# Two MLP phases of a hybrid backbone: sums of products nested in PSUM, stored operand combinations, and phase two product by product

## The chip, the core and the metric

The kernel runs on one core of a Trainium2 chip. The metric is the device time in microseconds (us) of one execution, as the median of three runs. TensorE (PE) multiplies, VectorE (DVE), ScalarE (ACT) and GpSimd (POOL) work element by element, and SyncE (SP) issues nearly all transfers between HBM and the on-chip SBUF, in the order of its own queue. PSUM is the memory in which TensorE accumulates.

## The reference, cut to what matters

Two layers over 1280 tokens (256 of a prompt, 1024 of a sample), width 1024, all in fp32. A layer is a mixer and an MLP with 4096 hidden units and a squared ReLU. Shift, scale and gate of either token group come from a modulation vector.

```python
def _modulation(cvec, w, b):
    m = jax.nn.silu(cvec) @ w + b
    return jnp.split(m[:, None, :], N_MOD, axis=-1)

def _mlp(h, w1, w2):
    return jnp.square(jax.nn.relu(h @ w1)) @ w2
...
        hp = _rmsnorm(xp, norm_mlp[l]) * (1.0 + mp[4]) + mp[3]
        hs = _rmsnorm(xs, norm_mlp[l]) * (1.0 + ms[4]) + ms[3]
        xp = xp + mp[5] * _mlp(hp, mlp_w1[l], mlp_w2[l])
        xs = xs + ms[5] * _mlp(hs, mlp_w1[l], mlp_w2[l])
    y_prompt = _rmsnorm(xp, norm_final)
    y_sample = _rmsnorm(xs, norm_final)
```

Layer 0 has the "even" mixer (windowed attention and a gated recurrence), layer 1 the "odd" one (Fourier and long convolutions). The change leaves both as they are, but for the order in which the odd mixer's first product takes its row tiles.

## The kernel before

**Precision.** Every large fp32 product is three products of rounded operands: an operand is split into `h` (rounded to fp32r) and `l` (the rest), and hh, hl and lh are summed. The split (L300, L303) is a cast on ScalarE and a subtraction on VectorE or GpSimd.

**Seven products.** Both matrix products of the MLP are cut into 2 x 2 blocks and done with seven block products instead of eight (Strassen-Winograd): "11", "21", "T1", "T2", "T3", "22" and "T4" name them, and also the combination of blocks that each one multiplies. One side's combinations are built from the activations, the other's from the weights (`wset`: additions on GpSimd in raw weight tiles `wr`, then `wtile` L802 splits each into `wt`). Weights are loaded as blocks of 512 KB into `wr`, of which there are two buffers, as there are of `wh` and `wl`.

**Phase 1** (L909 to L932), hidden activations: 16 steps j; each takes the seven products of 24 matmuls of 128 x 320 (`product`, L846), each product in a PSUM pair of its own. The sums of products are made outside of PSUM: ScalarE copies "11" and "T1" out (L857, L922), VectorE adds "21", "T2", "T3", "22" and "T4" (L860, L921, L924, L926, L929), GpSimd adds twice in SBUF (L923, L925). VectorE then squares the positive part of 1280 columns twice (L927, L930), and two rows of 640 KB go to the scratch `uscr`. A filler is pulled once per j: in layer 0 it is `modulation` for seven vectors, which multiplies rows of the modulation weights (`mt`) by the conditioning on VectorE, 224 instructions of L382 with a running sum.

**Phase 2** (L1021 to L1053), back to the width: seven chunks of 512 hidden units. For each, four rows `ur` are loaded back, `ops` builds and splits the seven combinations (tiles `o` and `oT`; additions on GpSimd, splits on ScalarE and VectorE), and for two halves `ms` of the columns the seven products run: 2 x 12 matmuls (L1034) into a PSUM pair each. Each pair is added to an accumulator `acc` in SBUF by VectorE (L1040). After the last chunk `merge` adds the seven accumulators up. The eighth chunk (512 hidden units) is a classic product (`proj`, L692), which adds into the residual `xm`; in layer 1 its columns go in two parts, with the final norm of the first part beside the second.

**What sets the order.** The program is written in the order in which loops and generators yield; a scheduler with a simulated timeline then sets the order of each engine's queue. Within a queue the instructions run in that order, and each waits for what its operands and its buffers need.

## Time and profile before

| | us |
|---|---|
| median of three runs | 3344.59 (3343.64 to 3347.43) |
| span of the profiled execution | 3345.9 |
| layer 0: steady part of phase 1 | 866 to 1240 |
| layer 0: phase 2 / classic chunk | 1261.6 to 1680 / to 1739.1 |
| layer 1: start and phase 1 | 2405.4 to 2846.8 |
| layer 1: phase 2 / classic chunk / tail | 2846.8 to 3264.7 / to 3327.8 / to 3345.9 |

| engine | busy us | share of the span |
|---|---|---|
| TensorE | 2960.5 | 88% |
| VectorE | 2512.5 | 75% |
| GpSimd | 1406.4 | 42% |
| ScalarE | 1225.1 | 37% |

Times within the kernel count from the start of the span. The shares are means over stages with different limits, so they don't tell which engine a stage waits for; for that the stages are read one by one, by windows, by the chain of waits and by what ended an engine's idle time. The granted clock of TensorE is 1.00 at its full 2.4 GHz; its mean over the span is 0.943.

### The profile page before, as it was taken

To read this page: it belongs to the slowest core of one execution; us is meant where nothing else is said; L and a number is where in the kernel's file an instruction comes from. 1 tells how busy PE (TensorE), PEld (TensorE's weight loads), DVE (VectorE), ACT (ScalarE), POOL (GpSimd) and SP (SyncE) were. 2 spreads that over 40 slices of the span, in tenths; PEclk is the share of its full clock that TensorE was granted. 3 is DMA by queue.
4 is the path that set the end of the run, shared out by engine and by line. 5 is a ranking of instruction groups with operands and counts; after the bars stand their busy time and mean duration, and the time that the engine had idled before them with its cause. 6 is when DMAs were issued, how large, how long until landed. Compare 5 with 4: busy or idle time off the path is not lost. (4 is left out here: it accounts for less than half of the span.)

```text
span 3345.9 us, 46730 instructions
## 1 busy us (share of the span) xinstructions
PE 2960.5 (88%) x18190; PEld 2716.9 (81%) x18190; DVE 2512.5 (75%) x3172; ACT 1225.1 (37%) x2032; POOL 1406.4 (42%) x912
## 2 busy tenths in 40 slices
PE   6799978897999998989799998887979999899977
PEld 3577767796988887989778876777979999898976
DVE  6886798648999987887983257875686656788896
ACT  5556757634111125333233332322432222533322
POOL 3530054524433336555630025543244344555563
PEclk8899989998999998999899998898989999999988
DMA  6363232341445443132331235546212223323232
GB/s 237 115 235 111 99 126 81 128 163 60 167 161 167 161 167 111 64 101 70 101 139 37 82 121 176 182 145 208 101 70 86 102 97 125 109 70 97 68 131 95
DMA packets 133336, 407.03 MB, mean 122 GB/s; under 512 B 14886, under 2 KB 29622, under 8 KB 133116
## 3 DMA queue, kind: packets, MB, share of 16 engines
q1 hardware_dynamic: 121596, 362.10, 31.6%
q0 software_dynamic: 11520, 41.95, 4.2%
q8 instruction: 144, 2.36, 0.3%
q14 instruction: 76, 0.62, 0.1%
HBM read 306.70 MB, written 97.29 MB: 121 GB/s over the span
## 5 line engine op out<-in xcount | busy, mean ns | idle before, releaser
L846 PE MATMUL pd<-BT,wt 128*128 128x320 f32 x3072 | 474.9, 314 | 42.5 <-ACT BT L764 21.6
L805 ACT CAST wt<-wr 128x512 fp32r<-128x512 f32 x360 | 221.2, 620 | 770.3 <-PE pd L1034 233.3
L846 PEld LDWEIGHTS pd<-BT,wt 128*128 128x128 f32 x3072 | 463.5, 192 | 48.1 <-ACT BT L764 22.6
L1034 PE MATMUL pd<-oT,wt 128*128 128x320 f32 x2688 | 427.8, 318 | 64.5 <-DVE acc L1040 54.5
L1034 PEld LDWEIGHTS pd<-oT,wt 128*128 128x128 f32 x2688 | 413.3, 195 | 72.7 <-issue 31.1
L846 PE MATMUL pd<-B,wt 128*128 128x320 f32 x2304 | 364.0, 315 | 35.2 <-DVE u L926 14.9
L846 PEld LDWEIGHTS pd<-B,wt 128*128 128x128 f32 x2304 | 349.4, 192 | 41.5 <-ACT wt L805 16.9
L1034 PE MATMUL pd<-o,wt 128*128 128x320 f32 x2016 | 324.7, 319 | 42.5 <-DVE acc L1040 25.8
L1034 PEld LDWEIGHTS pd<-o,wt 128*128 128x128 f32 x2016 | 310.5, 196 | 51.5 <-issue 24.6
L1040 DVE TENSOR_TENSOR acc<-acc,pd 128x640 f32<-128x640 f32 x336 | 270.2, 812 | 84.1 <-PE pd L1034 83.9
L300 DVE TENSOR_TENSOR wt<-wr,wt 128x512 fp32r<-128x512 f32 x276 | 265.8, 965 | 61.7 <-ACT wt L805 61.6
L923 POOL TENSOR_TENSOR u<-ut,u 128x640 f32<-128x640 f32 x32 | 55.0, 1719 | 413.0 <-ACT u L922 277.2
L300 POOL TENSOR_TENSOR ur<-ur 128x640 f32<-128x640 f32 x84 | 165.3, 1979 | 111.7 <-DVE o L300 69.5
L300 POOL TENSOR_TENSOR wt<-wr,wt 128x512 fp32r<-128x512 f32 x84 | 133.6, 1590 | 164.3 <-ACT wt L805 164.3
L300 POOL TENSOR_TENSOR wr<-wr 128x512 f32<-128x512 f32 x120 | 196.9, 1641 | 8.0
L692 PE MATMUL pb<-hh,wl 128*128 128x258 f32 (+1 forms) x720 | 191.9, 369 | 0.0
L692 PE MATMUL pb<-hh,wh 128*128 128x258 f32 (+1 forms) x720 | 191.5, 368 | 0.5 <-ACT hh L643 0.3
L692 PE MATMUL pb<-hl,wh 128*128 128x258 f32 (+1 forms) x720 | 191.5, 367 | 0.0
L303 ACT CAST wh<-wr 128x1024 fp32r<-128x1024 f32 x74 | 77.5, 1048 | 195.8 <-PE pd L692 79.8
L725 POOL TENSOR_TENSOR nacc<-nacc,nsq 128x640 f32<-128x640 f32 (+2 forms) x36 | 60.3, 1675 | 210.2 <-ACT nsq L724 210.1
L692 PEld LDWEIGHTS pb<-hh,wh 128*128 128x128 f32 x720 | 121.9, 190 | 27.9 <-issue 6.5
L692 PEld LDWEIGHTS pb<-hh,wl 128*128 128x128 f32 x720 | 121.9, 191 | 25.8 <-issue 6.0
(536 smaller groups left out, 6419.2 us busy)
## 6 DMA issues: line engine op xcount, KB each, us to landing
wr<-in_w_dram SPq DMA_DIRECT2D x136, 512.0 KB, 3.6
uscr<-u SPq DMA_DIRECT2D x64, 640.0 KB, 3.3
ur<-uscr SPq DMA_DIRECT2D x64, 640.0 KB, 4.9
tab<-in_dft_dram POOLq DMA_DIRECT2D x79, 512.0 KB, 4.7
mt<-in_mt_dram SPq DMA_DIRECT2D x112, 256.0 KB, 3.0
mw<-in_mw_dram SPq DMA_DIRECT2D x40, 512.0 KB, 4.7
x<-in_x_dram SPq DMA_DIRECT2D x16, 640.0 KB, 8.6
xmid<-x SPq DMA_DIRECT2D x32, 320.0 KB, 2.1
```

What stands on the lines that cost most here:

```text
L300: eng.tensor_tensor(o, x, y, ALU.subtract)
L303: S.copy(hi, src)
L692: T.matmul(ps[c][:, 0:N], w[wi][:, sl], hs[k][hi][:, c0:c0 + N], start=(ki == 0 and pi == 0), stop=(ki == nk - 1 and pi == 2))
L725: (V if last else G).tensor_tensor(s.acc[:, c0:c1], s.acc[:, c0:c1], sq, ALU.add)
L805: S.copy(t[:, 0], src)
L846: T.matmul(ps[:, c, 0:NQ], w[:, wi, 128 * k:128 * k + 128], B[n][k][:, hi_, NQ * c:NQ * c + NQ], start=(k == 0 and pi == 0), stop=(k == 3 ...
L923: G.tensor_tensor(u0[:, hi], t, u1[:, hi], ALU.add)
L1034: T.matmul(ps[:, z, 0:NQ], w[:, wi, sl], B2[n, k][:, hi_, NQ * z:NQ * z + NQ], start=(k == 0 and pi == 0), stop=(k == 1 and pi == 2))
L1040: V.tensor_tensor(d, d, ps[:, :, 0:NQ], ALU.add)
```

## The change

**Phase 1.** A product may be accumulated onto another one's PSUM pair (`onto`). The pair x takes "11", then "T2", "T3" and "T4" on top of it, and is read after each; z takes "T1" and then "22"; "21" has a pair of its own. VectorE adds "21", the sum after "T3" and the sum after "22"; ScalarE copies x after "11" and after "T2" and z after "T1", and takes the squared ReLU of two quarters in two passes (`act2`); VectorE squares the other two. The combinations that phase 2 multiplies are formed here (two subtractions on VectorE, two on GpSimd), and `keep` stores seven of them per j, 320 KB each, in `uscr`.

**Phase 2.** The loop goes product by product over all 4096 hidden units: eight steps `kk` for each of "11", "T2", "T3", "T4", "21", "T1" and "22". A step loads 640 KB of the stored combination, splits it (1280 elements a partition), loads one to three blocks of weights (T2: 3; T3 and T1: 2; the others: 1), combines them on GpSimd (in T2 also on VectorE), splits them (1024 elements) and runs 48 matmuls into four PSUM pairs, which are all of PSUM. "T2", "T3" and "T4" accumulate on "11", and "22" on "T1". After the eighth step of a product the four pairs are added to the residual through the gate (`addto`). `acc`, `merge` and the classic chunk are gone. In the last layer the squares for the final norm are taken in pieces, and the norm's end and the scaling of all eight tiles come after the last product, in two halves of 640 columns.

**Modulation** of the seven vectors goes to TensorE: 224 matmuls of 32 x 256 in fp32 and 56 that gather their rows, still as phase 1's filler in layer 0; its weights come in tiles of two per 512 KB, in the buffers of `tmp`, now six for four.

The three places in the engines' queues are these. A name in brackets is the engine or the DMA queue whose semaphore an instruction waits on; a number behind a name is that of its buffer.

TensorE in phase 1 of layer 1, a steady j, before: `BT2` and `BT1` are the operands of "T2" and "T1", `B21` that of "21", `pd` the PSUM pair.

```order
L846 MATMUL pd_23693<-B213_20211,wt_23594 128x320 x6
L846 MATMUL pd_23724<-BT20_20349,wt_23629 128x320 [waits DVE_49,Activation_49]
L846 MATMUL pd_23724<-BT20_20349,wt_23629 128x320 x5
L846 MATMUL pd_23724<-BT21_20359,wt_23629 128x320 x6
L846 MATMUL pd_23724<-BT22_20370,wt_23629 128x320 x6
L846 MATMUL pd_23724<-BT23_20380,wt_23629 128x320 x6
L846 MATMUL pd_23753<-BT10_20386,wt_23661 128x320 [waits Activation_49]
L846 MATMUL pd_23753<-BT10_20386,wt_23661 128x320 x3
L846 MATMUL pd_23753<-BT10_20386,wt_23661 128x320 [waits DVE_49]
L846 MATMUL pd_23753<-BT10_20386,wt_23661 128x320
```

After, the same place:

```order
L831 MATMUL pd_21326<-BT13_19990,wt_21225 128x320 x6
L831 MATMUL pd_21384<-B210_19780,wt_21293 128x320 [waits PE_49,Activation_49]
L831 MATMUL pd_21296<-BT20_19938,wt_21260 128x320 [waits Activation_49]
L831 MATMUL pd_21296<-BT20_19938,wt_21260 128x320 x3
L831 MATMUL pd_21296<-BT20_19938,wt_21260 128x320 [waits DVE_49]
L831 MATMUL pd_21296<-BT20_19938,wt_21260 128x320
L831 MATMUL pd_21296<-BT21_19948,wt_21260 128x320 x6
L831 MATMUL pd_21296<-BT22_19959,wt_21260 128x320 x6
L831 MATMUL pd_21296<-BT23_19969,wt_21260 128x320 x6
L831 MATMUL pd_21384<-B210_19780,wt_21293 128x320 x3
L831 MATMUL pd_21384<-B210_19780,wt_21293 128x320 [waits DVE_49]
```

Before, each product goes to a `pd` of its own, one after the other. Now "T2" goes onto the pair `pd_21296` that "11" filled, behind a wait for ScalarE's copy of it, and "T1" stands between the two; "21" has `pd_21384`.

VectorE within phase 2 of layer 1, before: L1040 empties PSUM, L300 splits the next chunk's operands.

```order
L1040 TENSOR_TENSOR acc<-acc,pd 128x640
L300 TENSOR_TENSOR oT_26848<-ur,oT_26848 128x640
L1040 TENSOR_TENSOR acc<-acc,pd 128x640
L300 TENSOR_TENSOR oT_26852<-ur,oT_26852 128x640
L300 TENSOR_TENSOR ur<-ur 128x640
L1040 TENSOR_TENSOR acc<-acc,pd 128x640
L300 TENSOR_TENSOR ur<-ur 128x640
L1040 TENSOR_TENSOR acc<-acc,pd 128x640
L300 TENSOR_TENSOR oT_26887<-ur,oT_26887 128x640
L1040 TENSOR_TENSOR acc<-acc,pd 128x640
L300 TENSOR_TENSOR oT_26893<-ur,oT_26893 128x640
```

After, in product "T2" of layer 1: `s` is the combination of weights, `ol` and `wt` the second parts of the splits.

```order
L295 TENSOR_TENSOR s_24395<-s_24395,wq 128x1024
L295 TENSOR_TENSOR wt<-s_24395,wt 128x1024
L295 TENSOR_TENSOR ol<-ur,oh 128x1280
L295 TENSOR_TENSOR s_24462<-s_24462,wq 128x1024
L295 TENSOR_TENSOR wt<-s_24462,wt 128x1024
L295 TENSOR_TENSOR ol<-ur,oh 128x1280
L295 TENSOR_TENSOR s_24529<-s_24529,wq 128x1024
```

Before, each addition out of PSUM stands behind a subtraction of the next chunk's operands. Within a product nothing is left that reads PSUM; the evacuations stand between two products.

SyncE within phase 2 of layer 1, before: `ur` are rows of activations, `wr` blocks of weights.

```order
L811 DMA wr_24602<-in_w2_dram 128x1024 [waits DMAHW5_49,Pool_49]
L811 DMA wr_24858<-in_w2_dram 128x1024 [waits DMAHW2_49,DVE_49]
L811 DMA wr_24860<-in_w2_dram 128x1024 [waits DMAHW3_49,Pool_49]
L979 DMA ur_25071<-uscr_100 128x1280 [waits DMAHW6_49,PE_49]
L979 DMA ur_25073<-uscr_100 128x1280 [waits DMAHW7_49,PE_49]
L979 DMA ur_25075<-uscr_100 128x1280 [waits DMAHW0_49,DVE_49,Pool_49]
L979 DMA ur_25077<-uscr_100 128x1280 [waits DMAHW1_49,DVE_49,Pool_49]
L811 DMA wr_25110<-in_w2_dram 128x1024 [waits DMAHW4_49,DVE_49]
```

After, in product "T2" of layer 1: `wq` is a third block of weights in another pool of buffers.

```order
L1014 DMA ur_24322<-uscr_99 128x1280 [waits DMAHW3_49,PE_49]
L955 DMA wq_24266<-in_w2_dram 128x1024 [waits DMAHW4_49]
L955 DMA wr_24262<-in_w2_dram 128x1024 [waits DMAHW1_49,Pool_49]
L955 DMA wr_24264<-in_w2_dram 128x1024 [waits DMAHW2_49]
L1014 DMA ur_24389<-uscr_99 128x1280 [waits DMAHW7_49,DVE_49,PE_49]
L955 DMA wq_24333<-in_w2_dram 128x1024 [waits DMAHW0_49]
L955 DMA wr_24329<-in_w2_dram 128x1024 [waits DMAHW5_49,Pool_49]
L955 DMA wr_24331<-in_w2_dram 128x1024 [waits DMAHW6_49]
```

Before, 4 loads of `ur` and 4 of `wr` serve a chunk of 336 matmuls. Now one `ur`, two `wr` and one `wq` serve a step of 48, and the first of two `wr` waits for GpSimd.

The diff, cut to its core:

```diff
+        for i in which:
+            mss = []
+            for jj in range(2):
+                ps = tbank()
+                for h in range(2):
+                    for kk in range(2):
+                        ws = []
+                        for z in range(2):
+                            w = tmp("mw", (128, 2, 256))
+                            ld(w.rearrange("p k c -> p (k c)"), a["mw"][l, 4 * i + 2 * jj + h, kk, :, 512 * z:512 * z + 512])
+                            ws.append(w)
+                        for g in range(4):
+                            T.matmul(ps[32 * g:32 * g + 32, 256 * h:256 * h + 256], st[:, 4 * kk + g, :], ws[g // 2][:, g % 2, :],
+                                     start=kk == 0, stop=kk == 1)
                         yield
-        for i in which:
-            m = mod[l][i]
-            V.tensor_tensor(m, macc[:, i, 0], macc[:, i, 1], ALU.add)
-            V.tensor_tensor(m, m, mb[:, l, 8 * i:8 * i + 8].unsqueeze(2).to_broadcast([128, 8, 2]), ALU.add)
-        yield
+                ms = tmp("ms")
+                S.copy(ms, ps)
+                mss.append(ms)
+            p2 = tbank()
+            for c in range(8):
+                T.matmul(p2[:, 2 * c:2 * c + 2], mss[c // 4][:, 128 * (c % 4):128 * (c % 4) + 128], sel, start=True, stop=True)
+            V.tensor_tensor(mod[l][i], p2[:, 0:16].rearrange("p (c s) -> p c s", s=2),
+                            mb[:, l, 8 * i:8 * i + 8].unsqueeze(2).to_broadcast([128, 8, 2]), ALU.add)
...
+        def product(n, w, onto=None):
+            ps = pbank() if onto is None else onto
...
+                                 start=(onto is None and k == 0 and pi == 0), stop=(k == 3 and pi == 2), skip_group_check=True)
...
+        def keep(n, j, src):
+            ld(uscr[UN[n], j // 2, :, j % 2], src)
+
+        def act2(dst, src):
+            S.activation(dst, src, AF.Relu)
+            S.activation(dst, dst, AF.Square)
+
+        def first(j, u0, w):
+            x = product("11", w)
+            S.copy(h1(u0), q2(x))
+            return x
+
+        def second(j, u0, w):
+            V.tensor_tensor(h1(u0), h1(u0), q2(product("21", w)), ALU.add)
+            act2(u0[:, lo], u0[:, lo])
+            keep("11", j, u0[:, lo])
...
+            u0 = u0s[j] if j < PRE else slot("u0", [128, NT], F32, "h")
+            x = xs[j] if j < PRE else first(j, u0, nextw())
+            u1 = slot("u1", [128, NT], F32, "gh"[j % 2])
+            z = product("T1", nextw())
+            S.copy(h2(u1), q2(z))
+            product("T2", nextw(), x)
+            S.copy(h2(u0), q2(x))
             if j >= PRE:
-                p11(t, nextw())
-                p21(t, u0, nextw())
-            u1 = slot("u1", [128, NT])
-            V.tensor_tensor(h1(t), h1(t), product("T2", nextw()), ALU.add)
-            S.copy(h2(u1), product("T1", nextw()))
-            G.tensor_tensor(u0[:, hi], t, u1[:, hi], ALU.add)
-            V.tensor_tensor(h1(t), h1(t), product("T3", nextw()), ALU.add)
-            G.tensor_tensor(u1[:, hi], t, u1[:, hi], ALU.add)
-            V.tensor_tensor(h2(u0), h2(u0), product("22", nextw()), ALU.add)
-            V.scalar_tensor_tensor(u0, u0, 0.0, u0, ALU.max, ALU.mult)
-            ld(uscr[2 * j], u0)
-            V.tensor_tensor(h1(u1), h1(t), product("T4", nextw()), ALU.add)
-            V.scalar_tensor_tensor(u1, u1, 0.0, u1, ALU.max, ALU.mult)
-            ld(uscr[2 * j + 1], u1)
+                second(j, u0, nextw())
+            product("T3", nextw(), x)
+            V.tensor_tensor(h2(u1), h2(u1), q2(x), ALU.add)
+            V.scalar_tensor_tensor(u1[:, hi], u1[:, hi], 0.0, u1[:, hi], ALU.max, ALU.mult)
+            keep("22", j, u1[:, hi])
+            product("22", nextw(), z)
+            V.tensor_tensor(h2(u0), h2(u0), q2(z), ALU.add)
+            V.scalar_tensor_tensor(u0[:, hi], u0[:, hi], 0.0, u0[:, hi], ALU.max, ALU.mult)
+            sub(V, u0[:, lo], u0[:, hi], u0[:, lo])
+            keep("T1", j, u0[:, lo])
+            sub(G, u0[:, hi], u1[:, hi], u0[:, hi])
+            keep("T3", j, u0[:, hi])
+            sub(V, u1[:, hi], u1[:, hi], u0[:, lo])
+            keep("T2", j, u1[:, hi])
+            product("T4", nextw(), x)
+            act2(h1(u1), q2(x))
+            keep("21", j, u1[:, lo])
+            sub(G, u1[:, lo], u1[:, lo], u1[:, hi])
+            keep("T4", j, u1[:, lo])
...
+        def weights(n, kk):
+            if n == "11":
+                return block(kk, A11)
+            if n == "21":
+                return block(kk, A12)
+            if n == "T4":
+                return block(kk, A22)
+            if n == "T2":
+                s2[kk] = slot("s2", [128, 1024])
+                p, q, r = block(kk, A21), block(kk, A22), block(kk, A11, "g")
+                G.tensor_tensor(s2[kk], p, q, ALU.add)
+                sub(V, s2[kk], s2[kk], r)
+                return s2[kk]
+            if n == "T3":
+                p, q = block(kk, A11), block(kk, A21, "g")
+                sub(G, q, p, q)
+                return q
+            if n == "T1":
+                p, q = block(kk, A21), block(kk, A22, "g")
+                G.tensor_tensor(q, p, q, ALU.add)
+                return q
+            p = block(kk, A12)
+            sub(G, p, p, s2[kk])
+            return p
+
+        def addto(m, ps, half):
+            x = xt[m]
+            if half:
+                V.scalar_tensor_tensor(h2(x), q2(ps), g[:, m, 1:2], h2(x), ALU.mult, ALU.add)
+                return
+            for z, z0, z1, si in ((0, 0, 256, 0), (0, 256, NQ, 1), (1, 0, NQ, 1)):
+                o = x[:, NQ * z + z0:NQ * z + z1]
+                V.scalar_tensor_tensor(o, ps[:, z, z0:z1], g[:, m, si:si + 1], o, ALU.mult, ALU.add)
...
+        for n in ("11", "T2", "T3", "T4", "21", "T1", "22"):
+            fresh = n in ("11", "21", "T1")
+            if fresh:
+                ps = [pbank() for _ in range(4)]
+            for kk in range(8):
+                ur = slot("ur", [128, 2, NH], F32, "h")
+                ld(ur, uscr[UN[n], kk])
+                o = [slot("o" + x, [128, 2, NH], F32R, "h") for x in "hl"]
+                split(ur, *o)
+                wt = weights(n, kk).rearrange("p (k c) -> p k c", k=2)
+                w = [wp.tile([128, 2, 512], F32R, tag="w" + x, name="wt") for x in "hl"]
+                split(wt, *w)
+                for mi in range(4):
+                    for k2 in range(2):
+                        for pi, (wi, oi) in enumerate(((0, 0), (0, 1), (1, 0))):
+                            for z in range(2):
+                                T.matmul(ps[mi][:, z, 0:NQ], w[wi][:, k2, 128 * mi:128 * mi + 128], o[oi][:, k2, NQ * z:NQ * z + NQ],
+                                         start=(fresh and kk == 0 and k2 == 0 and pi == 0), stop=(kk == 7 and k2 == 1 and pi == 2), skip_group_check=True)
+                    if kk == 7:
+                        addto(mi + 4 * (n in ("T3", "T4", "T1")), ps[mi], n in ("T2", "T3", "T1", "22"))
...
+        for m in range(4):
             if final:
-                break
-            for cpair in range(4):
-                w = wload(a["w2"][l, fc, cpair])
-                for c2 in range(2):
-                    m = 2 * cpair + c2
-                    if m == 2:
-                        merge(l, acc, xt, 1)
-                    ps = proj(w, 128 * c2, 256, us, NC, nk=4)
-                    update(ps, mod[l][5], m, xt[m], xt[m])
-                    norm_tile(nxt, m, xt[m])
+                ssq(m, NH, NT, False, V)
...
+            for c0, c1 in ((0, NH), (NH, NT)):
+                drain(rms_part(fin, c0, c1, slot("dg", [128, c1 - c0])))
                 for m in range(8):
                     x = xt[m][:, c0:c1]
+                    V.scalar_tensor_tensor(x, x, gn[:, 4, m:m + 1], fin.R[:, c0:c1], ALU.mult, ALU.mult)
                     ld(out["y"][m, :, c0:c1], x)
```

## Rows read from the trace of the kernel before

**Rows 1.** Groups by shape: count, busy us, mean ns, idle before, releasers
```profile
L1034 PE MATMUL pd<-oT,wt 128*128 128x320 f32 x2688 | 427.8, 318 | 64.5 <-DVE acc L1040 54.5 <-ACT acc L1038 10.0
...
L1034 PE MATMUL pd<-o,wt 128*128 128x320 f32 x2016 | 324.7, 319 | 42.5 <-DVE acc L1040 25.8 <-DVE u L929 15.6 <-ACT oT L303 1.1
...
L1040 DVE TENSOR_TENSOR acc<-acc,pd 128x640 f32<-128x640 f32 x336 | 270.2, 812 | 84.1 <-PE pd L1034 83.9
```

**Rows 2.** Windows: busy us (count) by engine, PEclk, DMA share, GB/s
```profile
866.00:1240.00 374.00, 341.90 (x2258) 335.55 (x2257) 352.16 (x629) 72.47 (x123) 135.78 (x81) 0.99 0.49 163
1261.60:1680.00 418.40, 368.59 (x2352) 359.87 (x2352) 351.46 (x353) 142.93 (x221) 250.63 (x143) 0.95 0.27 89
1680.00:1739.10 59.10, 58.12 (x288) 48.45 (x289) 46.91 (x55) 19.83 (x27) 22.96 (x7) 0.97 0.43 156
2405.40:2846.80 441.40, 407.95 (x2706) 404.09 (x2704) 289.00 (x284) 113.04 (x190) 196.18 (x115) 0.96 0.26 93
2500.00:2800.00 300.00, 300.00 (x2047) 300.00 (x2046) 180.18 (x170) 66.99 (x109) 122.59 (x72) 1.00 0.28 97
3264.70:3327.80 63.10, 61.38 (x304) 51.38 (x304) 41.03 (x55) 18.37 (x24) 24.53 (x13) 0.96 0.27 92
3327.80:3345.90 18.10, 3.52 (x13) 2.48 (x12) 8.53 (x17) 1.53 (x4) 2.43 (x2) 0.61 0.31 116
```

**Rows 3.** Chain, a chunk of layer 1's phase 2: start, us, tile
```profile
2969.13 25.55 PE pd L1034 x162
...
2999.14 0.81 DVE acc L1040
...
3014.34 3.21 DVE oT L300 x2
...
3026.36 25.53 PE pd L1034 x162
```

**Rows 4.** Modulation: groups of line L382 by shape; columns as in Rows 1
```profile
L382 DVE SCALAR_TENSOR_TENSOR mt<-mt,cb 128x512 f32<-128x512 f32 x112 | 110.3, 986 | 0.6
L382 DVE SCALAR_TENSOR_TENSOR mj<-mt,cb 128x512 f32<-128x512 f32 x112 | 105.3, 941 | 21.6 <-DMA mt<-in_mt_dram 21.6
```

**Rows 5.** PE's timeline early on: start, us, operation, records
```profile
52.15 0.95 PE L368 MATMUL pt<-c_sel,ms 128*128 128x2 f32 x8
...
58.96 1.50 PE L357 MATMUL pt<-mw,silu 128*32 128x256 f32 x24
```

**Rows 6.** Line L300 on VectorE: count, ns min/median/max, first, last start
```profile
L300 DVE TENSOR_TENSOR wt<-wr,wt x276: 673/684/3248, 769.0 to 3245.6; 128x512 fp32r<-128x512 f32 x138
...
L300 DVE TENSOR_TENSOR wl<-wr,wh x74: 1204/1216/3368, 217.0 to 3315.0; 128x1024 fp32r<-128x1024 f32 x74
```

**Rows 7.** The 1280-element subtraction on VectorE; columns as in Rows 1
```profile
L300 DVE TENSOR_TENSOR ul<-ur,uh 128x1280 fp32r<-128x1280 f32 x2 | 3.0, 1480 | 0.0
```

**Rows 8.** GpSimd's addition of 1024 elements; columns as in Rows 6
```profile
L542 POOL TENSOR_TENSOR fsq<-fsq x6: 2351/3022/3343, 55.3 to 166.0; 128x1024 f32<-128x1024 f32 x6
```

**Rows 9.** ScalarE's casts of 1024 and 1280 elements: columns as in Rows 6
```profile
L303 ACT CAST wh<-wr x74: 1031/1050/1057, 213.6 to 3313.3; 128x1024 fp32r<-128x1024 f32 x74
...
L303 ACT CAST uh<-ur x8: 1262/1262/1268, 1637.0 to 3239.5; 128x1280 fp32r<-128x1280 f32 x8
```

**Rows 10.** DMA issues of the page: count, KB each, us to landing
```profile
wr<-in_w_dram SPq DMA_DIRECT2D x136, 512.0 KB, 3.6
...
ur<-uscr SPq DMA_DIRECT2D x64, 640.0 KB, 4.9
```

**Rows 11.** SyncE's issue of a weight load; columns as in Rows 6
```profile
L811 SPq DMA_DIRECT2D wr<-in_w_dram x124: 327/332/333, 756.1 to 3206.6; - x124
```

**Rows 12.** The busiest DMA window, at phase 2's start; columns as in Rows 2
```profile
1272.00:1276.00 4.00, 0.00 (x0) 0.00 (x0) 4.00 (x5) 2.77 (x6) 1.98 (x1) 0.68 1.01 419
```

**Rows 13.** Timeline of the kernel's end
```profile
3331.09 1.40 PE L731 MATMUL pt<-ones,nacc 128*128 128x1 f32 x8 [3.21 <-DVE nacc L725]
...
3337.19 5.39 DVE L1079 SCALAR_TENSOR_TENSOR xm<-xm,c_gn,R 128x512 f32<-128x512 f32 x8 [2.52 <-ACT R L748]
```

266 lines of the change are left out of this document (65 added, 201 removed).

## The prediction

> **What bounds the kernel now.** I read the two MLP stages of each layer by windows first, to see whether TensorE is full there, then the groups by shape for what it waits on, then the chain of waits. A steady stretch of layer 1's phase 1 is TensorE's own: 2047 matmuls of 320 columns fill 300.00 us at a granted clock of 1.00, so 300.00 / 2047 = 146.5 ns each, and nothing else comes near (VectorE 180.18) [rows 2]. Layer 0's phase 1 is not: in 374.00 us TensorE is busy for 341.90, VectorE for 352.16 [rows 2], and 215.6 us of that stage's VectorE time are the modulation sums of L382 [rows 4]. There VectorE sets the pace.
>
> Phase 2 is bound by neither alone. Layer 0's chunks take 418.40 us with TensorE busy for 368.59 and the clock at 0.95 [rows 2]; at 146.5 ns its 2352 matmuls would be 344.6. TensorE's waits there end with the addition L1040 (54.5 and 25.8 us) and, at the entry of the phase, with L929 (15.6 for both layers, 7.8 each) [rows 1]. The chain shows why: after 162 matmuls in a row it runs through VectorE, where splits of the next chunk's operands (3.21 us for two oT) stand between the additions that free PSUM. The pattern repeats each 3026.36 - 2969.13 = 57.2 us [rows 3]; 336 matmuls at pace are 49.2, so about 8.0 us a chunk are lost, 56 in seven. The eighth chunk is the classic product: 59.10 us in layer 0, 63.10 in layer 1; behind it the last layer has a tail of 18.10 [rows 2].
>
> **The change, phase 2.** It takes away 168 additions per layer (336 of 812 ns in all [rows 1]), the merge, and the classic chunk. It adds matmuls: 7 products x 8 steps x 48 = 2688 per layer, for 2352 and 288 of the classic form. At pace that is 2688 x 146.5 ns = 393.9 us, 7.03 a step. I take the pace of phase 1, since a step's matmuls have the same shape and two of them share a weight load as there; nobody empties PSUM inside a product, so the wait on L1040 has nothing to sit on.
>
> What a step now asks of the others: ScalarE casts 1.26 + 1.05 = 2.3 us [rows 9]; VectorE subtracts 1.48 and 1.22, in T2 a further 1.22: 2.7 to 3.9 [rows 6, 7]; GpSimd combines weights in T2, T3, T1 and 22: 2.35 to 3.34 [rows 8]. All lie under 7.03. SyncE issues 2 to 4 loads at 0.33 [rows 11]. Bytes: T2 is the worst with 640 + 3 x 512 KB, 2.23 MB in 7.03 us or 317 GB/s, below the 419 that the busiest window moved [rows 12]. A ur load waits for the matmuls of some steps earlier, and in SyncE's queue weight loads stand behind it; it was issued three or four steps ahead, so 4.9 us to landing [rows 10] plus 2.7 of splitting is covered by two steps or more.
>
> One loop isn't covered. In T2 both wr buffers are freed by one GpSimd addition, and the next step's two loads are queued on it: 2 x 0.33 of issue, 3.6 to landing [rows 10, 11], then the addition, 2.35 to 3.34 [rows 8]: 6.6 to 7.6 us, and 8.6 if landing takes ur's 4.9. Against 7.03 over eight steps that is -0.4 to +1.6 each: 0 to 13 us, of which a lead of some us from the product before is spent first. I take 5. In T3, T1 and 22 the buffers alternate, so the same sum stands against two steps.
>
> Between products the accumulators are read by 28 evacuations, each near the 0.8 us of L1040 [rows 1]; the three nested changes must wait for them, but only 12 matmuls wait for one. Six changes at 0 to 1.5, taken as 0.7: 4 us. Phase 2 is then 393.9 + 5 + 4 = 403. For the entry, 7.8 before, the chain left behind the last product of phase 1 is two ScalarE passes, a store and the first load's remainder; the first products' operands are stored earlier, so 0.7 to 6, and I take 3.
>
> *Layer 1*: phase 1 ends at 2846.8 - 7.8 = 2839.0. After: 2839.0 + 3 + 403 = 3245 where before the classic chunk ended at 3327.8.
>
> **The tail** grows. Before, from the column sums at 3331.09 to the first scaling at 3337.19 are 6.1 us, eight scalings take 5.39, and 3.3 are left to the end [rows 2, 13]. After, all of it lies behind the last product: last addition, square and sum 3 x 0.75 = 2.3 (each near L1040's 0.81 [rows 1]), 6.1 for the chain and about 2 more as two halves go through it, 16 scalings of 640 at 5.39 / 8 x 640 / 512 = 0.84, 13.5, and 3.3: 27 us. Ends: 20, if the first half's scalings hide in the second's chain, and 31. I take 28.5, as the halves' chains stand together in the order. Layer 1 ends at 3273.5: a gain of 72.4.
>
> *Layer 0*: before, 1739.1 - 1261.6 = 477.5 from phase 2's start, and its next stage begins at 1739.1. After: 1253.8 + 3 + 403 = 1660, and 3 for the last norm pieces that the odd mixer's first product waits for (0 to 8): 1663. A gain of 76.
>
> **The change, phase 1.** Products per j stay seven. VectorE loses two additions and half of the 1280-element squarings, and gains two subtractions of 640; ScalarE gains four passes of 640. From 180.18 and 66.99 in 300 [rows 2], neither gets near full. The T-products now wait for ScalarE's or VectorE's read of the same accumulator, but the order puts a product of 24 (3.5 us) between, against a read of about 0.8. Seven stores of 320 KB replace two of 640: 2.3 for 1.3 MB per j. That adds some 40 GB/s to 97 [rows 2]. Layer 1's phase 1: 0, from -2 to +10.
>
> In layer 0 the modulation goes from VectorE to TensorE: 224 products of 32 x 256 at 1.50 / 12 = 0.125 us (two records to one instruction) are 28 us, 56 sums at 0.95 / 4 = 0.24 are 13 [rows 5]. The steady window's 2258 matmuls at pace are 331; 331 + 41 = 372 for 374.00. A mw tile waits for a buffer freed by VectorE and GpSimd right ahead of its use: 0 to 1 us per j, so I add 6. A loss of 4; ends: a gain of 10 (part of the products in earlier gaps) and a loss of 20.
>
> **The sum**: 72.4 + 76 - 4 = 144. The profiled span is 3345.9; of the three runs only that of 3347.43 is longer, so 1.5 us lie around it if it is that one. 3345.9 - 144 = 3202, and the median lies 1.3 under the span: **3201 us**.
>
> **The rivals.** (a) *GpSimd and VectorE hold each other up.* VectorE's split of 1024 took 1.22 in the median but 3.37 at worst, 2.15 more, which is less than one GpSimd addition [rows 6, 8]. Then T2's addition waits for a running split (up to 1.5), the loop is 8.1 to 10.1, and eight steps lose 9 to 25; with the clock at phase 2's present 0.95 for the four combined products (393.9 x 4/7 x 0.05 = 11) a layer is some 25 longer: 3201 + 50 = 3251, still faster. Against it: the median is the undisturbed value.
>
> The Trainium skill, SBUF — State Buffer, "SBUF: two separate sides", states a rule that speaks against this change: a VectorE instruction with two SBUF inputs and a GpSimd instruction that reads SBUF exclude each other, and the second waits for the whole of the first. The worst case above agrees with it, and by it (a) is the outcome, 3251, where the sum by the medians gives 3201.
>
> (b) *Everything hides*: the T2 loop at its 6.6, changes at 0, the tail at 20, modulation at its gain. 2 x 9 + 8 + 14 = 40 less: 3161; half of it, 3180, is as far as I believe.
>
> (c) *Slower: each step waits for its own loads.* If a ur load, held by TensorE's end of an earlier step, comes so late that the weight loads behind it in SyncE's queue start only when the step before ends, a step is 0.66 + 3.6 + 1.05 + 3.37 = 8.7 and up to 10 with 4.9 to landing. The gain of 148 in 112 steps is gone at 7.03 + 1.32 = 8.35 us a step; at 9.2 the time is 3201 + 112 x 2.2 = 3447. Against it: the queue shows ur three or four steps ahead. For it: SyncE issues in order, and here 88 weight blocks a layer go through two buffers where before there were 32.
>
> (d) *The 8 us a chunk were never the additions'* but the splits', and come back under another name: eight chunks at 57.2 are 457.6 for 403: 3201 + 2 x 54.6 = 3310.
>
> **How the numbers follow.** Forecast (3180 to 3225) 0.56, (a) 0.20, (b) 0.10, (c) 0.07, (d) 0.05, and 0.02 for no gain at all. 0.2% is 6.7 us, about what a measurement of this kernel tells from no change. Faster 0.91, same 0.02, slower 0.07. Forecast, (a) and the upper half of (b) make the range 3170 to 3265; outside are (c), (d) and the rest, with some of (b).
>
> **What would show it.** Right: phase 2 at about 403 us a layer, matmuls near 146.5 ns, clock near 1.00, TensorE's waits on VectorE gone but at product changes; T2 the only product over 57 us; 28 us behind the last product; layer 0's phase 1 as long as before with TensorE full. Wrong: waits of TensorE on DMA or on splits in every step (c), long VectorE splits beside GpSimd's additions in four products (a), L1040's 8 us turning up under another line (d), or phase 1 slower by its stores.

## The result, and the profile after

The changed kernel takes 3254.39 us in the median (3246.62 to 3255.83) where the kernel before takes 3344.32 in the same comparison: a ratio of 0.9726, interval 0.9712 to 0.9739 (the ratio is taken over the runs, not from the two medians). It is 90 us faster. The prediction was 3201 (3170 to 3265), a gain of 143: right in sign and within the range, but its sum promised 1.6 times the gain that came. Its rival (a) had named 3251; whether for the right reason is a question below.

Cut at the first matmul of each stage, the two profiled executions stand so (us; the predicted column is the prediction's own sum, laid out by stage). Only layer 0's phase 2 is cut behind its last matmul, so that TensorE's wait before the odd mixer counts with the mixer; the 3 us that were forecast for it stand there too:

| stage | before | predicted | after | after less predicted |
|---|---|---|---|---|
| up to layer 0's phase 1 | 774.7 | 774.7 | 780.5 | +5.8 |
| layer 0: phase 1 | 486.9 | 486 | 510.3 | +24 |
| layer 0: phase 2 (and classic chunk) | 477.5 | 403 | 412.1 | +9 |
| odd mixer | 666.3 | 669.3 | 675.2 | +6 |
| layer 1: phase 1 | 441.4 | 437 | 438.8 | +2 |
| layer 1: phase 2 (and classic chunk) | 481.0 | 403 | 408.4 | +5 |
| tail | 18.1 | 28.5 | 26.0 | -3 |
| span | 3345.9 | 3202 | 3251.3 | +50 |

The windows of the changed kernel, whose columns are those of [rows 2], show the same stages from inside:

```profile
780.50:1290.80 510.30, 482.83 (x3265) 432.07 (x3263) 233.34 (x294) 168.29 (x277) 158.11 (x105) 0.97 0.51 175
870.00:1240.00 370.00, 370.00 (x2558) 330.60 (x2557) 147.76 (x190) 116.03 (x188) 110.67 (x77) 1.00 0.52 177
1290.80:1702.90 412.10, 400.51 (x2688) 397.66 (x2688) 232.69 (x184) 141.24 (x133) 108.92 (x38) 0.99 0.63 213
2816.90:3225.30 408.40, 400.37 (x2688) 396.81 (x2688) 220.23 (x174) 137.09 (x127) 118.39 (x44) 0.99 0.60 205
2991.00:3048.00 57.00, 57.00 (x391) 57.00 (x390) 24.87 (x21) 19.09 (x17) 0.00 (x0) 1.00 0.53 167
3225.30:3251.30 26.00, 7.79 (x30) 5.51 (x28) 18.73 (x34) 2.95 (x8) 0.00 (x0) 0.63 0.53 202
```

Phase 2 is TensorE's now: 400 of 408 to 412 us busy at a granted clock of 0.99, and VectorE's load has fallen from 84% [rows 2] to 54 and 56%. A product without combined weights runs at 57.00 / 391 = 145.8 ns a matmul (the row in which TensorE is busy for all of 57.00 us). What surprised is the second row: in layer 0's phase 1 TensorE is busy for the whole 370.00 us, VectorE for 147.76, and yet the phase is longer than before, when VectorE was the one that was full.

**Where layer 0's phase 1 went.** TensorE's timeline, with start, duration and records:

```profile
1005.09 0.62 PE L371 MATMUL pt<-mw,silu 128*32 128x256 f32 x4
1005.64 0.71 PE L831 MATMUL pd<-BT,wt 128*128 128x320 f32 x3
...
1053.23 1.49 PE L371 MATMUL pt<-mw,silu 128*32 128x256 f32 x20
1054.65 1.58 PE L831 MATMUL pd<-B,wt 128*128 128x320 f32 x9
...
1106.27 0.63 PE L371 MATMUL pt<-mw,silu 128*32 128x256 f32 x6
1106.83 3.79 PE L831 MATMUL pd<-BT,wt 128*128 128x320 f32 x24
...
1168.49 1.07 PE L371 MATMUL pt<-mw,silu 128*32 128x256 f32 x16
1169.49 0.71 PE L831 MATMUL pd<-B,wt 128*128 128x320 f32 x3
```

Two records are one instruction. From the start of a group of the modulation's matmuls (L371) to the start of the next product's matmuls are 0.55 us for two instructions and 0.56 for three; six (1023.48 to 1024.46) took 0.98 and eight 1.00; nine (1110.54 to 1111.96) and ten took 1.42. These are steps: each started round of four instructions costs about 0.43 us, however many of the four there are, and the group some 0.13 beside. The four instructions of a round write the four quarters of PSUM's partitions. In the order 58 of the 73 groups of L371 are pairs, since a tile of 256 KB holds only two of the four row blocks and the scheduler sends each pair off when its tile is there; a pair pays for four. Added up from start to start, the 73 groups take 48 us (90 rounds, where 224 instructions in full rounds would be 56), and 112 records of the sums at 0.87 / 8 (1028.70 to 1029.57) are 12 more: some 60, where the prediction had 28 + 13 = 41. Its row of twelve instructions [rows 5] was three full rounds.

The Trainium skill, TensorEngine Tiling (Array Packing), "Tiling Modes", says that matmuls of 32 weight columns run in four independent tiles of the array and that a change of the tiling mode drains TensorE. The steps of four agree with the first; whether the 0.13 us of a group are such a drain no run here shows.

**Phase 2's loop in T2.** The chain of waits through product "T2" of layer 1, with start and duration:

```profile
2888.60 4.28 DMA wr<-in_w_dram
...
2893.04 2.58 POOL s L970
2895.63 0.33 SPq L955
...
2896.01 4.64 DMA wr<-in_w_dram
...
2900.80 2.41 POOL s L970
2903.23 0.33 SPq L955
...
2939.12 171.07 PE pd L1024 x1147
```

This is the loop that the prediction named: issue, landing, GpSimd's addition, and again. One round, 2895.63 to 2903.23, takes 7.6 us; the others take 7.3 to 7.4, but for one of 8.3 and a first one of 10.4, whose landings take 5.3 and 6.6. The addition is at 2.4 to 2.6, near its lower bound, but for one of 3.2; the landing is otherwise 4.3 to 4.6, not 3.6. Behind T2 and T3's first step TensorE goes 1147 records without a wait.

**Two waits that had been put down to something else.** In layer 0's last product the norm of the next stage begins. VectorE's and GpSimd's timelines, and TensorE's waits:

```profile
1642.03 3.19 DVE L636 SCALAR_TENSOR_TENSOR hl<-xm,cf,hh 128x1024 fp32r<-128x1024 f32 x1
1645.14 2.89 DVE L295 TENSOR_TENSOR hl<-mod,hh 128x2 fp32r<-128x2 f32 x1
1647.96 4.30 DVE L636 SCALAR_TENSOR_TENSOR hl<-xm,cf,hh 128x256 fp32r<-128x256 f32 x2
...
1652.25 1.21 DVE L295 TENSOR_TENSOR wt<-wr,wt 128x1024 fp32r<-128x1024 f32 x1
```

```profile
1639.92 11.25 POOL L626 TENSOR_TENSOR nsq<-nsq 128x1280 f32<-128x1280 f32 x3
```

```profile
1653.51 1.43 PE L1024 MATMUL pd<-oh,wt 128*128 128x320 f32 x4 [6.91 <-DVE wt L295]
...
1710.90 1.41 PE L684 MATMUL pb<-hh,wh 128*128 128x258 f32 x3 [8.00 <-DVE xm L988]
```

A subtraction of two columns takes 2.89 us while GpSimd adds three times in a row; the one at 1652.18, behind them, takes 0.15. The split for which TensorE waits (1652.25) stands behind these in VectorE's queue. The same happens at the stage's end, where the last evacuation is late by 7 us and the odd mixer's first product with it. Neither wait costs its length alone. Behind each the granted clock of TensorE is at or near the lower of its levels, 1.2 GHz, for 5 and 6 us:

```profile
1653.50:1658.50 5.00, 4.99 (x19) 4.99 (x20) 5.00 (x7) 0.00 (x0) 1.17 (x1) 0.50 0.68 236
1711.00:1717.00 6.00, 6.00 (x18) 4.98 (x19) 6.00 (x6) 2.58 (x4) 3.03 (x4) 0.54 0.27 109
```

The 19 and 18 matmuls in them are some 2.8 and 3.5 us of work at 146.5 ns and at the 0.58 us for three that the odd mixer's next products take (from 1717.02 on), so each wait costs over 2 us more.

### The profile page after: what moved, and what is told of

It is laid out like the page before. It is cut to its first block, busy times and chain, and to the rows that moved or that the text cites. A ratio compares the mean times of both kernels' runs of the same rounds, so it can differ in the third digit from the quotient of the medians.

```text
span 3251.3 us, 47128 instructions
## 1 busy us (share of the span) xinstructions
PE 2973.1 (91%) x18846; PEld 2718.9 (84%) x18846; DVE 1914.1 (59%) x2266; ACT 1286.9 (40%) x1960; POOL 1010.6 (31%) x674
## 5 line engine op out<-in xcount | busy, mean ns | idle before, releaser
L1024 PE MATMUL pd<-oh,wt 128*128 128x320 f32 x3584 | 681.2, 311 | 19.1 <-ACT wt L298 8.8
L1024 PEld LDWEIGHTS pd<-oh,wt 128*128 128x128 f32 x3584 | 565.8, 189 | 25.1 <-ACT wt L298 13.2
L831 PEld LDWEIGHTS pd<-BT,wt 128*128 128x128 f32 x3072 | 459.7, 190 | 31.4 <-issue 18.1
L1024 PE MATMUL pd<-ol,wt 128*128 128x320 f32 x1792 | 410.6, 310 | 1.5 <-DVE ol L295 1.5
L295 DVE TENSOR_TENSOR wt<-wr,wt 128x512 fp32r<-128x512 f32 (+1 forms) x256 | 230.3, 901 | 301.8 <-ACT wt L797 273.7
L295 DVE TENSOR_TENSOR ol<-ur,oh 128x1280 fp32r<-128x1280 f32 x112 | 195.1, 1743 | 246.3 <-PE pd L1024 200.5
L1024 PEld LDWEIGHTS pd<-ol,wt 128*128 128x128 f32 x1792 | 302.3, 189 | 1.9 <-DVE ol L295 1.8
L298 ACT CAST oh<-ur 128x1280 fp32r<-128x1280 f32 x112 | 141.4, 1263 | 339.4 <-DMA ur<-uscr 336.3
L797 ACT CAST wt<-wr 128x512 fp32r<-128x512 f32 x192 | 118.7, 620 | 170.9 <-PE pd L831 145.8
L684 PEld LDWEIGHTS pb<-hl,wh 128*128 128x128 f32 x720 | 123.0, 191 | 26.3 <-issue 6.7
L306 PE MATMUL pb<-arh,tab 128*128 128x512 f32 x288 | 115.3, 426 | 25.6 <-ACT arh L298 16.2
```

The lines of the kernel that those rows point to most:

```text
L295: eng.tensor_tensor(o, x, y, ALU.subtract)
L298: S.copy(hi, src)
L306: T.matmul(ps, w, m, start=(i == 0), stop=(i == n - 1))
L684: T.matmul(ps[c][:, 0:N], w[wi][:, sl], hs[k][hi][:, c0:c0 + N], start=(ki == 0 and pi == 0), stop=(ki == nk - 1 and pi == 2))
L797: S.copy(t[:, 0], src)
L831: T.matmul(ps[:, c, 0:NQ], w[:, wi, 128 * k:128 * k + 128], B[n][k][:, hi_, NQ * c:NQ * c + NQ], start=(onto is None and k == 0 and pi == ...
```

## Experiments

Ratios are to the kernel before; the changed kernel's is 0.9726. A difference of 0.001 is 3.3 us.

**Pairs or fours.** In the filler, a tile holds four row blocks of 128 columns:

```diff
-                            w = tmp("mw", (128, 2, 256))
+                            w = tmp("mw", (128, 4, 128))
...
-                            T.matmul(ps[32 * g:32 * g + 32, 256 * h:256 * h + 256], st[:, 4 * kk + g, :], ws[g // 2][:, g % 2, :],
+                                T.matmul(ps[32 * g:32 * g + 32, c0:c0 + 128], st[:, 4 * kk + g, :], w[:, g, :],
```

> The changed kernel, with one edit in the modulation filler: a tile of 256 KB holds four row blocks of 128 columns instead of two of 256, so that the four matmuls that go to the four quarters of PSUM's partitions come from one tile and stand together. Theory P (TensorE's time in layer 0's phase 1 is what the modulation costs, and a pair of its matmuls takes as long as four): the 448 records of the modulation took 0.55 us per pair, some 62 us; by fours of half the width about 0.27 per tile, 30 us. Phase 1 of layer 0 falls from 510 us to about 480, the kernel from 3254 to about 3225 (3215 to 3235). Rival W (it is the wait for tiles and buffers that costs, not TensorE's time): the loads are as many and as large, so no more than 5 us change, 3249 to 3259.

Measured: 3240.49 us, ratio 0.9690 (0.9675 to 0.9704), 12 us faster; layer 0's phase 1 went from 510.2 to 498.8. The direction is theory P's, the size less than half of what it gave. Its rows say why:

```profile
995.26 0.43 PE L370 MATMUL pt<-mw,silu 128*32 128x128 f32 x8
995.62 1.30 PE L830 MATMUL pd<-BT,wt 128*128 128x320 f32 x7
...
1000.05 0.65 PE L370 MATMUL pt<-mw,silu 128*32 128x128 f32 x16
1000.62 1.59 PE L830 MATMUL pd<-BT,wt 128*128 128x320 f32 x9
```

Four instructions of half the width take 0.36, not 0.27, and eight 0.57: a round costs 0.21, half of what it did, and the group's 0.14 or so remains. That a pair takes as long as four was right; that all 112 pairs stood alone, and that the group had no price of its own, was not. Added up, the 64 groups take 36 us for 48, and 11 to 12 is what the phase and the kernel gained.

**The filler's price.** The modulation's products are left out:

```diff
-            yield from modulation(0, (5,))
-            yield from modulation(1, (1, 0, 2, 4, 3, 5))
+            for l, i in ((0, 5), (1, 1), (1, 0), (1, 2), (1, 4), (1, 3), (1, 5)):
+                V.tensor_copy(mod[l][i], mb[:, l, 8 * i:8 * i + 8].unsqueeze(2).to_broadcast([128, 8, 2]))
+            yield
```

> The changed kernel without the products of the modulation in phase 1's filler: the seven vectors are set to their bias, so their weights are neither loaded nor multiplied (224 matmuls, 56 sums, 112 loads left out). This measures what the filler costs. Theory P (all of it is TensorE's time, in a stretch where TensorE is busy throughout): the stretch from 870 us to the end of phase 1 falls from 421 to about 345 us, the kernel to about 3180 (3172 to 3190). Rival W (it lies beside other waits): 3215 to 3245.

Measured: 3175.35, ratio 0.9491 (0.9472 to 0.9510); phase 1 of layer 0 takes 438.4 us, as long as layer 1's 439.0. The seven vectors cost 71.8 us of the phase, all of it in the open. This is theory P (72 for the 76 that it gave the stretch). Of the 72, some 60 are explained by the groups and sums above; the other 12 aren't told apart.

**Modulation back on VectorE.** The filler of the kernel before in the changed kernel:

```diff
-                            T.matmul(ps[32 * g:32 * g + 32, 256 * h:256 * h + 256], st[:, 4 * kk + g, :], ws[g // 2][:, g % 2, :],
-                                     start=kk == 0, stop=kk == 1)
+                        V.scalar_tensor_tensor(j if s_ == 0 else w, w, 1.0, cb[:, s_], ALU.mult, ALU.mult,
+                                               accum_out=macc[:, i, hf, c, s_:s_ + 1])
```

> The changed kernel with its modulation undone: the seven vectors are multiplied on VectorE again, as in the kernel before. Theory P (VectorE, relieved of PSUM additions, would have had room): VectorE is busy for some 168 us between 870 and 1291 us; 216 us of products, 18 of read-outs and 4 of sums make 406 in a stretch of which TensorE would need 345, so this stretch is bound by VectorE at about 406 to 415 instead of 421: 3240 (3225 to 3255). Rival (moving the modulation to TensorE was what phase 1 of layer 0 needed): VectorE's queue delays the reads of PSUM, the stretch grows past 430, 3265 to 3290.

Measured: 3229.71, ratio 0.9656 (0.9642 to 0.9671), 23 us faster than the changed kernel, and 10 better than expected. Phase 1 of layer 0 takes 490.7. VectorE is busy for 89% of a window in the phase (870 to 1200), and it is VectorE that TensorE waits for, as the longest of its waits between 870 and 1264 shows (us in all, times, longest):

```profile
870.00:1200.00 330.00, 302.95 (x1968) 297.38 (x1967) 292.66 (x550) 102.30 (x164) 114.59 (x70) 0.97 0.58 195
```

```profile
PE pd L838 <- DVE u L928: 26.9, 13, 3.3
```

So this part of the change was a loss: once phase 1's sums nest in PSUM, VectorE has room for most of the modulation, and TensorE has none. But nesting alone won nothing in this phase either: with the same filler the kernel before took 486.9. The wait above is on the sum after "T3" (L928), which has to be read before "T4" may go onto the same pair. Product "22" stands between, 3.5 us, and where the read stands behind modulation in VectorE's queue that isn't enough, by up to 3.3 us.

**T2's raw blocks.**

```diff
-                p, q, r = block(kk, A21), block(kk, A22), block(kk, A11, "g")
+                p, q, r = block(kk, A21), block(kk, A22, "g"), block(kk, A11, "g")
```

> The changed kernel with one of T2's two raw weight blocks loaded into the other pool, so that a step of T2 needs one of the two wr buffers and not both. Theory L (in T2 the loop of issue, landing and GpSimd addition, 7.4 to 7.8 us a step by the chain of waits, is what TensorE waits for): T2 goes at 7.03 a step, the waits on the splits in T2 and at its end go, 6 to 10 us a layer, 3254 to about 3238 (3232 to 3246). Rival D (the transfers themselves limit T2, at 306 GB/s): the wait moves to the landing of the same bytes, 3250 to 3258. Rival G (VectorE and GpSimd hold each other up): unchanged as well, with long splits beside the additions.

Measured: 3237.84, ratio 0.9684 (0.9669 to 0.9698), 14 us faster. Layer 1's chain, in place of the loop:

```profile
2817.86 273.26 PE pd L1024 x1862
```

From 10 us into phase 2 TensorE runs 1862 matmuls, nearly five of the seven products, without a wait, T2 among them, while the bytes are the same. Rival D and rival G fall: what T2 waited for was two buffers freed by one addition. Layer 1's phase 2 went from 408.1 to 398.6 between its first and last matmul, layer 0's from 411.8 to 408.0.

**The odd mixer's 8 us.** The norm of the last four tiles is held until the last evacuation is issued:

```diff
-                norm_tile(nxt, m, xt[m])
+                with tc.issue_after(last.ins):
+                    norm_tile(nxt, m, xt[m])
```

> The changed kernel with the norm of the last four tiles of layer 0 held back until the last evacuation of the MLP has been issued. Theory Q (TensorE's 8.0 us before the odd mixer are an evacuation that stands in VectorE's queue behind normalizing operations, each held up by a GpSimd addition): the evacuation comes 5 us earlier and the gap falls to about 3: 3249 (3246 to 3252). Rival (the first product waits for the normalized tiles, whatever the order): the gap stays 7 to 9, 3252 to 3257.

Measured: 3246.16, ratio 0.9705 (0.9689 to 0.9722). The intervals overlap, so the total decides nothing; the wait itself does:

```profile
1707.90 0.82 PE L684 MATMUL pb<-hh,wh 128*128 128x258 f32 x3 [1.07 <-DVE xm L988]
```

8.00 us became 1.07 (3 were expected). It was an evacuation that stood in a queue, not the norm that the first product reads.

**Sums of squares on VectorE.**

```diff
-            G.tensor_tensor(s.acc, s.acc, sq, ALU.add)
+            E.tensor_tensor(s.acc, s.acc, sq, ALU.add)
...
-                        norm_tile(nxt, 4 + i, xt[4 + i])
+                        norm_tile(nxt, 4 + i, xt[4 + i], E=V)
...
-                norm_tile(nxt, m, xt[m])
+                norm_tile(nxt, m, xt[m], E=V)
```

> The changed kernel with one edit: the sums of squares of layer 0's norm, behind and within its last MLP product, are added up on VectorE and not on GpSimd. Theory X (VectorE's operations take two to twenty times as long while GpSimd adds: a subtraction of two columns took 2.89 us beside three additions of 11.25, and TensorE then waited 6.9 us in product 22 and 8.0 before the odd mixer): VectorE gets eight operations of 1.48 more and yet both waits shrink, 6.9 to below 2 and 8.0 to 2 to 4: 3254 to about 3243 (3238 to 3248), and operations on VectorE in that stretch are at their usual durations. Rival (VectorE is simply overloaded there by the norm): with 12 us more of work the waits grow: 3255 to 3268.

Measured: 3239.86, ratio 0.9683 (0.9668 to 0.9697), 14 us faster with more work on VectorE. Its timeline at the end of the stage:

```profile
1700.71 1.28 DVE L636 SCALAR_TENSOR_TENSOR hl<-xm,cf,hh 128x1024 fp32r<-128x1024 f32 x1
1701.90 0.16 DVE L295 TENSOR_TENSOR hl<-mod,hh 128x2 fp32r<-128x2 f32 x1
1701.97 0.88 DVE L988 SCALAR_TENSOR_TENSOR xm<-pd,mod,xm 128x640 f32<-128x640 f32 x1
1702.77 1.49 DVE L626 TENSOR_TENSOR nsq<-nsq 128x1280 f32<-128x1280 f32 x1
```

The 1024-column operation takes 1.28 for 3.1 to 3.2, the two-column one 0.16 for 2.89, and the odd mixer's wait is 2.2. The waits on splits in product "22" fell less than expected, from 6.9 us to one of 0.6 and one of 3.4. Theory X holds, the overload falls.

**Evacuations put back.** Each step of phase 2 starts and empties its four PSUM pairs:

```diff
-                                         start=(fresh and kk == 0 and k2 == 0 and pi == 0), stop=(kk == 7 and k2 == 1 and pi == 2), skip_group_check=True)
-                    if kk == 7:
+                                         start=(k2 == 0 and pi == 0), stop=(k2 == 1 and pi == 2), skip_group_check=True)
+                    if True:
```

> The changed kernel without the nesting over the contraction in phase 2: each step starts its four PSUM pairs anew and empties them into the residual (the sums of products are then not those of the reference, the work is). This undoes the part that took the additions away and leaves the order by products and the stored combinations. Theory N (what phase 2 gained is that nobody empties PSUM within a product): VectorE has four evacuations of 0.88 to 1.3 more per step beside 2.7 to 3.9 of splits, the pairs come free late, and a step takes 8 to 9.5 us for 7.2: 3254 + 100 to 250 = 3350 to 3500. Rival O (the gain is of the stored combinations and the order by products; the evacuations hide behind the other three pairs): 3254 to 3290.

Measured: 3276.01, one run (the kernel before 3344.5): 22 us slower than the changed kernel. Theory N, which had 100 to 250, fails by a factor of five or more, and rival O's range holds the time. Layer 1's phase 2 from its first to its last matmul:

```profile
2831.00:3248.50 417.50, 402.57 (x2687) 396.79 (x2688) 393.99 (x537) 136.86 (x126) 116.90 (x44) 0.99 0.59 200
```

VectorE is busy for 94%, more than in the kernel before [rows 2], and empties as many pairs per matmul, four per 48. Phase 2 takes 417.5 us for 408.1 between first and last matmul, and 430.4 for 411.8 in layer 0; TensorE's waits on evacuations, 10.4 and 18.8 us, are as much. So the number of evacuations wasn't what cost the kernel before its 8 us a chunk. Was it the evacuations at all? That was asked of the kernel before:

```diff
-                            V.tensor_tensor(d, d, ps[:, :, 0:NQ], ALU.add)
+                            S.copy(d, ps[:, :, 0:NQ])
```

> The kernel before with one edit: what empties PSUM in phase 2 is ScalarE's copy, not VectorE's addition (so the sums over the chunks are left out; PSUM is read as often). Theory B (the 8 us lost in each chunk are PSUM pairs that wait for a VectorE that splits the next chunk's operands at the time): the evacuations no longer stand behind splits, a chunk goes from 57.2 to 50 to 52, and the two phases 2 gain 35 to 50 each: 3344 to 3245 to 3275. Rival D (the splits come late themselves, for they wait for buffers that the running chunk holds): the wait moves to the operands, 3320 to 3340.

Measured: 3263.93, ratio 0.9753 (0.9733 to 0.9772), 83 us faster than the kernel before. The stretches without a wait, a chunk apart, in its chain:

```profile
2913.09 28.63 PE pd L1034 x192
...
2965.76 26.70 PE pd L1034 x180
```

A chunk takes 52.7 us for 57.2 [rows 3]; phase 2 of layer 1 falls from 413.5 to 373.3 between first and last matmul. Theory B holds for most of the loss. The edit also takes work off VectorE, so windows have to say whether that was it. The kernel before splits the next chunk's operands in the second half of a chunk alone (`pull(g2)` where `ms` is 1). The first and the second half of a chunk, in the kernel before and in this one, in the columns of [rows 2]:

```profile
2969.00:2995.00 26.00, 25.87 (x166) 25.90 (x167) 17.03 (x22) 4.02 (x7) 8.95 (x7) 0.93 0.30 92
3000.00:3026.00 26.00, 21.47 (x138) 19.98 (x136) 26.00 (x25) 10.44 (x17) 21.08 (x12) 1.00 0.27 92
...
2913.00:2939.00 26.00, 25.91 (x175) 25.73 (x176) 12.05 (x9) 17.25 (x30) 16.52 (x12) 1.00 0.37 142
2940.00:2966.00 26.00, 25.10 (x169) 24.57 (x168) 23.82 (x17) 19.41 (x31) 20.42 (x11) 1.00 0.13 41
```

In the second half VectorE is full before (26.00 of 26.00) and nearly full still (23.82), and GpSimd beside it as busy (21.08, 20.42); yet TensorE gets from 21.47 to 25.10 us. So it had not waited for the splits themselves: the pairs were late because their evacuations stood in VectorE's queue behind a burst of splits. Take the evacuations out of that queue, as here, and most of the wait is gone: in layer 1 TensorE's waits on L1040 fall from 39.1 us to 5.1. Spread the splits over the steps, as in the run before, and most of it is gone too, though there GpSimd also has less to do (116.90 us of 417.50, for 250.63 of 418.40 in layer 0 before [rows 2]), and VectorE's splits beside GpSimd are longer. The changed kernel does both, and of the two the even steps seem to carry more: putting the evacuations back cost 28 us in two phases that had lost some 112. Splits spread evenly in the kernel before itself weren't tried, so that share is argued, and GpSimd's lighter load remains a rival for a part of it.

**Two versions put together.** First, four vectors on VectorE and three on TensorE (tiles of four by 128), with T2's block and the sums of squares:

> The changed kernel with four edits: of the seven modulation vectors four on VectorE as before and three on TensorE with tiles of four row blocks by 128 columns; in T2 one of two raw blocks in the other pool; layer 0's sums of squares on VectorE. Theory: the first stage's stretch has VectorE at about 168 + 135 = 303 us and TensorE at 345 + 26, so it is TensorE's at about 375 for 421: -45; T2 -14; the norm -11: 3254 to about 3184 (3172 to 3200). Rival (the edits take from one another, or the filler of two kinds collides on the four small buffers): 3205 to 3230.

Measured: 3206.93, ratio 0.9588 (0.9572 to 0.9604). Phase 1 of layer 0 took 486.2 us, not 465: TensorE is full again (322.41 of 330), waits 7.0 us for tiles of the modulation's weights, and phase 2 began with a wait of 7.0 for ScalarE's cast of its first weights. So the rival came true: the three edits apart, with all of the modulation on VectorE (-23, -14, -14), add up to about as much. Then with no modulation on TensorE, but spread:

```diff
-            pull(filler, 4)
+            pull(filler, 2)
...
+                if n != "22" and kk % 2:
+                    pull(late)
...
-            yield from modulation(1, (1, 0, 2, 4, 3, 5))
+            yield from modulation(1, (1, 0, 2))
...
+        def fill3():
+            yield from modulation(1, (4, 3, 5))
```

> The changed kernel with the modulation back on VectorE, but spread: four vectors as phase 1's filler at half the rate per step, three within layer 0's phase 2 (two tiles in every second step of six products); also T2's second raw block in the other pool and layer 0's sums of squares on VectorE. Theory S (TensorE sets both phases as long as VectorE has room: 148 + 136 of some 350 us in phase 1, 233 + 102 of 405 in phase 2): phase 1 of layer 0 falls from 510 to about 445, phase 2 stays at 405 to 415, with -14 and -11 for the two other edits: 3254 - 65 - 25 = 3164 (3155 to 3185). Rival Q (VectorE's work is in the way wherever it stands, since evacuations and splits queue behind it): phase 2 of layer 0 grows by 20 or more and phase 1 stays near 480: 3195 to 3220.

Measured: 3189.35, ratio 0.9535 (0.9519 to 0.9551): 64 us faster than the changed kernel, the best of those that compute the whole, but outside the 3155 to 3185 of theory S, and below rival Q's 3195. Its two stages:

```profile
775.00:1221.00 446.00, 408.56 (x2704) 404.62 (x2702) 355.57 (x533) 160.46 (x262) 176.88 (x105) 0.95 0.49 172
1221.00:1651.00 430.00, 408.95 (x2688) 403.75 (x2688) 309.43 (x405) 141.44 (x134) 92.17 (x34) 0.97 0.69 239
```

Phase 1 takes 446, as theory S had it (445), for 510.3. Phase 2 takes 430 where 405 to 415 were expected: with VectorE at 309.43 TensorE waits there 13.0 us for VectorE's part of the splits and 12.6 for ScalarE's, so Q is right there for about 20 us.

## Why the prediction was right and where it failed

- **What bounds before**: right for phase 2 (pairs that wait for L1040, shown by the kernel with ScalarE's copies). But "nobody empties PSUM inside a product" was taken as what makes TensorE run at pace. With the evacuations put back it runs nearly so. The reading of the chain was right (splits between additions); what the runs show in place of the number of evacuations is where they stand in VectorE's queue. Rival (d), that the 8 us would come back under another name, did not happen. For phase 1 of layer 0 VectorE's load alone is not the bound that it was taken for: with nested sums and the modulation on VectorE, VectorE is busy there for 421.36 us instead of 449.47, and the phase still takes 490.7 for 486.9.
- **Phase 2 at 403**: 412.1 and 408.4. Pace right (145.8 for 146.5). T2's loop was the right mechanism; its round is mostly 7.3 to 7.6 by a landing of 4.3 to 4.6, and it cost more than the 5 taken in layer 1 and about that in layer 0, within the 0 to 13 given: the kernel that frees it gains 9.5 and 3.8 between the first and the last matmul of the two phases. In layer 0 the 6.9 us in product "22", and the clock behind them, were in no term. The weight load that two matmuls were to share played no part: the windows count as many loads as matmuls.
- **Entry and product changes**: TensorE's wait at the entry is below 1 us in both layers, for 3. At product changes its waits on evacuations come to 0.6 in layer 0, where 4 a layer were taken.
- **Tail**: 26.0 for 28.5. The sixteen scalings take 12.82 for 13.5.
- **Layer 0's phase 1**: the step that failed, +24 of the 50. Two things were wrong in it. The 41 us were priced by a row in which twelve instructions stood together [rows 5], three full rounds of four, while the order has pairs, each of which takes as long as four; some 60 came of it, and the whole filler measured 72. And the 372 for 374 was called a draw, which hid that a stage that VectorE bounds gains nothing if the work that is taken off it is laid on TensorE, which is full at once. Where both are near full, an exchange has to be priced per unit on both sides: 7.5 us a vector on VectorE in the open (490.7 - 438.4 over seven), 10.3 on TensorE.
- **Layer 1's phase 1**: 438.8 for 437, right. A product of 24 between a nested product and the read before it is enough in its steady steps, where TensorE waits for no such read; in layer 0, with modulation in VectorE's queue, it isn't (26.9 us).
- **The odd mixer**: +9 for +3. The wait had been taken for the norm's last pieces; it was an evacuation behind them in VectorE's queue, and the clock was low for 6 us behind it.
- **Rival (a)** has the measured time by chance. VectorE and GpSimd do hold each other up, but not in T2, where it was placed: GpSimd's additions there were at 2.4 to 2.6 but for one of 3.2, VectorE's splits at 1.22 and 1.49, and the loop was long by its landings. In layer 1's T3 and T1 the splits of weights did stretch, to means of 1.63 and 2.36, as (a)'s sign had it, but TensorE lost only 1.2 us by one of them. The cost came in the last product of layer 0, with the norm's additions. The rows there agree with the Trainium skill's rule (SBUF — State Buffer, "SBUF: two separate sides"): the two-column subtraction takes nearly as long (2.83 to 2.89) as one of GpSimd's additions (6.01 for two, at 1700.12). What it cost there, with GpSimd adding without a pause, is the 14 us that the sums on VectorE gained. Rival (c) did not come; of the 88 blocks that it sent through two buffers, 24 go to `wq`.
- **The start**, 5.8 us later than before, was in no term. The edits of the order there are few; the kernels of the experiments begin phase 1 between 774.8 (no modulation products) and 782.0 (sums of squares on VectorE), though their edits lie behind that point. The scheduler lays out each kernel anew; which of its moves costs the 6 us stays open.

## What to carry to other kernels

Price a moved matmul by the company in which the new order puts it, not by a row where it stands among its like: here two matmuls of 32 weight columns cost as much as four, and each group that broke into a stream of another shape a little more. A wait on an evacuation is a matter of what stands ahead of it in its engine's queue at that moment; look at that before counting the evacuations. And where a change moves work from a full engine to one that will then be full, try the same work in the stage that has become slack.
